# Dilated attention scores in one run over four PSUM banks, and the denominators as a full-array product

## The chip, the core and the metric

The kernel runs on one core of one Trainium2 chip. A core has TensorE (PE, matrix products), VectorE (DVE), ScalarE (ACT), GpSimd (POOL) and SyncE (SP), whose queue here issues the DMAs. The metric is the device time of one execution in microseconds; a profiled execution gives the trace that is read below. Lower is better.

## What is computed

A two-layer encoder trunk over 512 tokens of width 1024, all in float32. Each layer makes one big input projection, then three token mixers (a gated recurrence, a dilated sliding-window attention with 8 heads, a latent attention), gates, projects and merges them. The change touches the dilated attention alone. Cut to what matters:

```python
def _dilated_group(q, k, v, slopes, window, dilation):
    ...
    s = jnp.einsum('brnqhd,brnkhd->brhnqk', qb * (Dh ** -0.5), kb) + bias
    s = jnp.where(allowed, s, MASK_VALUE)
    m = jnp.max(s, axis=-1, keepdims=True)
    p = jnp.exp(s - m)
    den = jnp.sum(p, axis=-1, keepdims=True)
    o = jnp.einsum('brhnqk,brnkhd->brhnqd', p, vb) / den
    lse = (m + jnp.log(den))[..., 0]
    ...
def _dilated_mixer(qkv_groups):
    ...                          # three groups: dilation 1, 4 and 16
    w = jax.nn.softmax(jnp.stack(lses), axis=0)
    o = jnp.sum(w[..., None] * jnp.stack(outs), axis=0)
```

The softmax over the three groups means that one common maximum and one common denominator per query and head are enough.

## The kernel before

The projections (`in_fm`, `mm3`, line L300) keep features on the 128 partitions and 512 tokens on the free axis. A weight tile of 128 columns is loaded by SP (L280), ACT casts it to a high half (`w_...h`, L274), POOL subtracts to get the low half (`w_...l`, L275), and PE makes three passes of eight 128x512 products (`xh,h`, `xl,h`, `xh,l`). Two raw tiles and three split tiles are in flight.

The dilated stage runs over four head pairs, hp0 to hp3, in each of two layers: eight units. The main loop issues, for each pair, the scores (`dil_scores`), then the projections of the next pair (`dl`, or after hp3 the latent attention's `cq`, `ckv`, `kr` from `mla_compress`), then the exponentials (`dil_exp`), some of the merge (`br`, L1089, with the merge gates `mg`), and the values (`dil_values`).

In `dil_scores` a head has 64 features, so the two heads of a pair sit in the two halves of the partitions and their products use 64 rows of the array each (`dsa`, L927, for the first group; `dsb`, L951, for the other two). The products of the two heads are issued in turn, and go to two PSUM banks. DVE then adds the position table and takes the row minimum (L898), which leaves scores in `za`, `zb` and minima in the small tile `dst`. There are four such runs a unit: two for `dsa`, two for `dsb`, each of eight to sixteen 64-row passes (a float32 product counts as two), each after the minima that free its banks (`after(first, reads[-2])`).

The minima of the two sides have other token orders. So they are written to DRAM (`da` L984, `db` L974) and read back as `dso` (L985, L986, and L976 to L978), all on SP's queue. `dil_exp` takes the minimum of `dst` and `dso` (L993, DVE) and then makes 16 exponentials on ACT (L999, L1004). `dil_values` transposes them (`dta`, `dtb`), multiplies by the values into the output bank (`do`, L1019, two heads in two column halves of the array), and makes `dn` (L1063): the reciprocals of the denominators are spread over the partitions by a product with the identity, 64 columns for each head. Then `yb` = dn x gate x do (DVE).

PSUM has three pools here: four banks `mm` for the projections, three banks `at` (`at_bank`) for scores, transposes, `dn` and the norm broadcasts (`hgrb`, `cqrb`, L546), and one output bank (`o_bank`). Behind hp3 stands the norm of `cq`: `cqms` (L536, mean square by product), an inverse square root on DVE in three Newton steps (`rsqrt`, L261 to L267, tile `cqrs0y` or `cqrs1y` by layer), and `cqrb`, which spreads it over the partitions on PE.

The order of the instructions on each engine isn't the order of the code. A scheduler places them by a simulated timeline (`schedule_with_timeline_sim=True`), and `after(a, b)` adds an order between two instructions. A change of one stage can so move the work around it.

Of the kernel before, what the change touches and what calls it, by code (L numbers as in the profile page):

```python
# [195 lines left out]
def bcast(ap, dims):  # L196
    return bass.AP(ap.tensor, ap.offset, [list(ap.ap[0])] + [list(d) for d in dims])
# [3 lines left out]
def tile_encoder(ctx: ExitStack, tc: tile.TileContext, x, xt, positions, blocks, wuq, wuh, par_in, brow, lbp,  # L201
# [259 lines left out]
    def layer(l, x_src, need_next):  # L461
# [361 lines left out]
        def hgrn_pair(hp, parts, v):  # L823

            o = o_bank(f"ho{hp}_{l}")
            n = 0
            for w in range(NT):
                ws = slice(w * 128, w * 128 + 128)
                for what in range(3):
                    if (what == 1 and w == 0) or (what == 2 and w == 3):  # L830
                        continue
                    for i, (a, s, qq, ready) in enumerate(parts):
                        if what == 0:
                            c = 128 * hp + 64 * i
# [12 lines left out]
            sq = t2(f"hsq{hp}_{l}", tag="acc")  # L847
            A.activation(sq, o, AF.Square, scale=1.0 / KEY_SCALE)
            if hp == 0:
                squares.append(sq)  # L850
            else:
                V.tensor_tensor(squares[0], squares[0], sq, ALU.add)
            return oc
# [31 lines left out]
        def dil_scores(hp, qk):  # L885

            q0, k0, q1, k1, q2, k2 = qk
            sl = slopes()
            stat = sm.tile([128, 2, 2, 4], F32, tag="dst", name=f"dst{hp}_{l}")
            other = sm.tile([128, 2, 2, 4], F32, tag="dso", name=f"dso{hp}_{l}")  # L890
            za = [fap(t4(f"za{hp}{i}_{l}", tag="a4"), 0, [[1, 1024]]) for i in range(2)]
            zb = [fap(t4(f"zb{hp}{i}_{l}", tag="a4"), 0, [[1, 1024]]) for i in range(2)]
            tab_mid = con[:, O_MID:O_MID + 256]
            tab_end = con[:, O_END:O_END + 128]
            tab_b = con[:, O_G12:O_G12 + 256]

            def biased_min(dst, ps, tab, slope, acc):
                return V.tensor_tensor_reduce(dst, ps, tab, float(slope), 3.0e38, ALU.add, ALU.min, acc)  # L898


            pr = [slice(64 * i, 64 * i + 64) for i in range(2)]
            reads = []

            def pair(name, products, minima):
                sc = [at_bank(f"{name}{i}_{l}") for i in range(2)]
                first = products(sc)
                if reads:
                    after(first, reads[-2])
                if len(reads) > 2:
                    after(first, reads[-3])  # L910
                for i in range(2):
                    reads.append(minima(i, sc[i]))

            def products_a(jp):
                def go(sc):
                    first = None
                    for j in (2 * jp, 2 * jp + 1):
                        o_ = [t[:, (j % 2) * 256:(j % 2) * 256 + 256] for t in sc]
                        if j < 3:
                            ops = [(slice(0, 128), 256, slice(64 + 128 * j, 192 + 128 * j),  # L920
                                    slice(128 * j, 128 * j + 256))]
                        else:
                            ops = [(slice(0, 64), 128, slice(448, 512), slice(384, 512)),
                                   (slice(64, 128), 128, slice(0, 64), slice(0, 128))]
                        for rows, wd, qs, ks in ops:
                            for i in range(2):
                                m = nc.tensor.matmul(o_[i][rows, :wd], q0[pr[i], qs], k0[pr[i], ks], start=True,  # L927
                                                     stop=True)
                                first = first or m
                    return first  # L930
                return go

            def minima_a(jp):
                def go(i, ps):
                    for j in (2 * jp, 2 * jp + 1):
                        wd = 256 if j < 3 else 128
                        last = biased_min(za[i][:, 256 * j:256 * j + wd],
                                          ps[:, (j % 2) * 256:(j % 2) * 256 + wd], tab_mid if j < 3 else tab_end,
                                          sl[2 * hp + i], stat[:, 0, i, j:j + 1])
                    return last  # L940
                return go

            def products_b(rp):
                def go(sc):
                    first = None
                    for r in (2 * rp, 2 * rp + 1):
                        rs = slice(128 * r, 128 * r + 128)
                        for g, (q_, k_) in enumerate(((q1, k1), (q2, k2))):
                            c = (r % 2) * 256 + 128 * g
                            for i in range(2):  # L950
                                m = nc.tensor.matmul(sc[i][:, c:c + 128], q_[pr[i], rs], k_[pr[i], rs], start=True,  # L951
                                                     stop=True)
                                first = first or m
                    return first
                return go

            def minima_b(rp):
                def go(i, ps):
                    for r in (2 * rp, 2 * rp + 1):
                        last = biased_min(zb[i][:, 256 * r:256 * r + 256],  # L960
                                          ps[:, (r % 2) * 256:(r % 2) * 256 + 256], tab_b, sl[8 + 2 * hp + i],
                                          stat[:, 1, i, r:r + 1])
                    return last
                return go

            for jp in range(2):
                pair(f"dsa{hp}{jp}", products_a(jp), minima_a(jp))
            da = dram.tile([2, 576], F32, tag="da", name=f"da{hp}_{l}")
            db = dram.tile([2, 512], F32, tag="db", name=f"db{hp}_{l}")
            by_residue(da, stat, other)  # L970
            for rp in range(2):
                pair(f"dsb{hp}{rp}", products_b(rp), minima_b(rp))

            nc.sync.dma_start(db.rearrange("i (p r) -> p i r", r=4), stat[:, 1])  # L974
            for i in range(2):
                nc.sync.dma_start(other[:, 0, i, 0:3], db[i, 64:448].rearrange("(j p) -> p j", p=128))  # L976
# [33 lines left out]
        def dil_values(hp, exps, vs, gate, behind):  # L1010
# [46 lines left out]
            d = V.tensor_tensor(den[:, 1], den[:, 1], other[:, 1], ALU.add)  # L1057
            after(d, *copies)
            V.reciprocal(den[:, 1], den[:, 1])
            dn = at_bank(f"dn{hp}_{l}")  # L1060
            for r in range(4):
                for i in range(2):
                    nc.tensor.matmul(dn[64 * i:64 * i + 64, slice(r, None, 4)],  # L1063
                                     bcast(den[:, 1, i, r:r + 1], [[0, 64]]), ident, start=r == 0, stop=r == 3,
                                     skip_group_check=True)
            y = t2(f"yb{hp}_{l}")
            V.tensor_tensor(y, dn, gate, ALU.mult)
            V.tensor_tensor(y, y, o, ALU.mult)
            return split(y, f"yb{hp}{l}")


# [229 lines left out]
```

## Time and profile before

| | us |
|---|---|
| median of three runs | 1773.09 (1772.72 to 1774.57) |
| the profiled execution | 1771.63 |
| its span, granted TensorE clock | 1769.9, 0.996 |
| PE busy | 1741.8 (98%), 10616 matmuls |
| DVE, ACT, POOL busy | 1064.2 (60%), 730.3 (41%), 573.8 (32%) |
| DMA | 154.15 MB, mean 87 GB/s |

A row of the timeline gives the start in the span, the time of that group, the engine, the line, the operation with out<-in, shapes (rows*columns of the array, then partitions x elements), and in brackets the idle time of the engine before it with what ended it. Matmuls are pipelined: a row's time runs to the end of the last product, so the distance of two starts is the better price. PEld is PE's weight load, SPq is SP's DMA queue. "x16" counts passes. Tile names are without buffer numbers.

### The profile page before, as it was taken

What the parts mean: (1) busy time and instruction counts of PE and PEld (TensorE: products, weight loads), DVE (VectorE), ACT (ScalarE), POOL (GpSimd) and SP (SyncE); (2) the same over time, 40 slices, a digit from 0 to 9 for tenths busy, and PEclk for the clock granted to TensorE, in tenths of its full rate; (3) what the DMA queues carried; (4) which work ended last, traced back from release to release, by engine and by line L of the source; (5) the groups of instructions that cost most, each with busy time, mean ns of one, the idle gap of its engine ahead of it and who ended that gap; (6) DMA issues with size and microseconds to landing.
All of it is one profiled execution on the core that took longest, in us unless ns stands there. A gap on an engine that the chain in (4) does not pass through costs nothing. (4 is left out here: it accounts for less than half of the span.)

```text
span 1769.9 us, 26458 instructions
## 1 busy us (share of the span) xinstructions
PE 1741.8 (98%) x10616; PEld 1450.5 (82%) x10616; DVE 1064.2 (60%) x1912; ACT 730.3 (41%) x1273; POOL 573.8 (32%) x338
## 2 busy tenths in 40 slices
PE   9999999999999999999999999999999999999997
PEld 7778978988888888887888888888888888888876
DVE  8888777443232566756777778775333324666576
ACT  6445454242424353433254455442424254444330
POOL 0412244233333233333213212532433332433341
PEclk9999999999999999999999999999999999999999
DMA  5223222223222222332332222222223221324221
GB/s 194 84 66 102 73 73 89 73 72 96 79 77 84 70 75 79 113 111 72 119 114 90 84 78 74 89 78 78 72 72 98 82 83 48 99 67 151 72 86 69
DMA packets 77146, 154.15 MB, mean 87 GB/s; under 512 B 37728, under 2 KB 37856, under 8 KB 77024
## 3 DMA queue, kind: packets, MB, share of 16 engines
q1 hardware_dynamic: 77024, 152.47, 27.9%
q8 instruction: 83, 1.36, 0.3%
q14 instruction: 39, 0.32, 0.1%
HBM read 148.15 MB, written 4.29 MB: 86 GB/s over the span
## 5 line engine op out<-in xcount | busy, mean ns | idle before, releaser
L775 DVE TENSOR_TENSOR kk<-kk,fr 128x512 f32<-128x512 f32 x96 | 94.0, 999 | 30.0 <-ACT kc L745 18.9
L696 POOL TENSOR_TENSOR qq<-hq,fr 128x1024 f32<-128x1024 f32 x16 | 42.5, 2654 | 201.6 <-DVE fr L689 181.9
L774 DVE TENSOR_TENSOR qq<-qq,fr 128x512 f32<-128x512 f32 x96 | 75.3, 797 | 16.9 <-POOL qq L696 15.2
L1079 DVE TENSOR_SCALAR mg<-mg 128x512 f32<-128x512 f32 x32 | 53.2, 1669 | 49.0 <-ACT mg L1078 48.9
L898 DVE CUSTOM_DVE_ANT_0 zb<-dsb,con 128x256 f32<-128x256 f32 x64 | 23.3, 421 | 46.4 <-PE dsb L951 46.3
L767 DVE COPY_PREDICATED ha<-mask,hs 64x256 f32<-64x256 uint8 (+1 forms) x80 | 40.4, 505 | 16.7 <-PE hs L757 15.6
L275 POOL TENSOR_TENSOR wb_1l<-wb_1r,wb_1h 128x1024 fp32r<-128x1024 f32 x12 | 29.5, 2460 | 63.6 <-ACT wb_1h L274 42.5
L275 POOL TENSOR_TENSOR wb_0l<-wb_0r,wb_0h 128x1024 fp32r<-128x1024 f32 x12 | 29.5, 2461 | 63.4 <-ACT wb_0h L274 42.4
L881 DVE TENSOR_SCALAR dl<-dl,par,con 128x512 f32<-128x512 f32 x24 | 25.8, 1075 | 38.0 <-PE dl L300 37.9
L735 POOL TENSOR_SCALAR_AFFINE_SELECT ha<-hc 128x256 f32<-128x256 f32 x32 | 13.8, 456 | 105.0 <-ACT hc L730 97.3
L658 ACT COPY mpt<-mtr 128x128 f32<-128x128 f32 x64 | 17.0, 266 | 74.4 <-DVE mpt L658 74.4
L757 PEld LDWEIGHTS hs<-qq,kc 128*64 128x64 f32 x1024 | 33.1, 137 | 16.2 <-issue 8.4
L999 ACT ACTIVATE za<-za,dst 128x256 f32<-128x256 f32 x64 | 30.0, 470 | 33.2 <-DVE dst L993 33.2
L757 PE MATMUL hs<-qq,kc 128*64 128x64 f32 x1024 | 38.0, 225 | 4.3 <-DVE qq L774 4.3
L716 POOL TENSOR_TENSOR hk<-kk,f 128x256 f32<-128x256 f32 x32 | 24.8, 775 | 51.5 <-DVE fr L778 51.5
L792 ACT COPY hkt<-hkt 128x384 f32<-128x384 f32 x32 | 15.3, 480 | 59.9 <-PE hkt L790 59.6
L745 ACT COPY kc<-kk 128x512 f32<-128x512 f32 x64 | 37.5, 618 | 4.6 <-DVE kk L775 4.6
L658 DVE COPY mpt<-mtr 128x128 f32<-128x128 f32 x64 | 18.4, 288 | 32.7 <-PE mtr L655 22.3
L1079 DVE TENSOR_SCALAR mgc<-mgc 128x512 f32<-128x512 f32 x16 | 22.9, 1429 | 22.3 <-ACT mgc L1078 22.3
L1099 DVE TENSOR_TENSOR acc<-acc,mgc 128x512 f32<-128x512 f32 x16 | 32.2, 2049 | 0.0
L662 PE MATMUL mo<-mpt,mv 128*128 128x128 f32 (+1 forms) x192 | 31.9, 309 | 0.0
L1004 ACT ACTIVATE zb<-zb,dst 128x256 f32<-128x256 f32 x64 | 31.6, 495 | 0.0
(1509 smaller groups left out, 5400.8 us busy)
## 6 DMA issues: line engine op xcount, KB each, us to landing
wb_0r<-in_blocks_dram SPq DMA_DIRECT2D x12, 512.0 KB, 3.6
wb_1r<-in_blocks_dram SPq DMA_DIRECT2D x12, 512.0 KB, 3.6
w_0r<-in_blocks_dram SPq DMA_DIRECT2D x9, 512.0 KB, 3.4
w_1r<-in_blocks_dram SPq DMA_DIRECT2D x8, 512.0 KB, 3.6
w_2r<-in_blocks_dram SPq DMA_DIRECT2D x8, 512.0 KB, 3.5
w_3r<-in_blocks_dram SPq DMA_DIRECT2D x8, 512.0 KB, 3.6
wo_0r<-in_blocks_dram SPq DMA_DIRECT2D x8, 512.0 KB, 3.6
wo_1r<-in_blocks_dram SPq DMA_DIRECT2D x8, 512.0 KB, 3.5
```

The source lines that it names most:

```text
L275: (eng or nc.gpsimd).tensor_tensor(lo, raw, hi.bitcast(F32), ALU.subtract)
L658: (A.copy if kb % 2 else V.tensor_copy)(pts[kb][:, qs], tr[:, kb * 128:kb * 128 + 128])
L662: nc.tensor.matmul(o[:, cols], v[:, kb, h * 128:h * 128 + 128], pts[kb][:, cols], start=qt == 1 and kb == 0, stop=qt == NT - 1 and kb == N ...
L696: nc.gpsimd.tensor_tensor(qq, bcast(q, [[0, 2], [1, S]]), fr, ALU.mult)
L745: made = A.copy(fap(kc, 0, [[2 * m, R // 2], [m, 2], [1, m]]), fap(kk, 0, [[2 * m, R // 2], [S + m, 2], [1, m]]))
L757: mat = nc.tensor.matmul(sc[rows, to], kc[:, at], rhs, start=True, stop=True)
L767: ready = [V.copy_predicated(fap(a[rows], cols.start, [[128, NT], [1, wd]]), bcast(mk, [[0, NT], [1, wd]]), fap(sc[rows], cols.start, [[12 ...
L774: V.tensor_tensor(fap(qq, 0, dims), fap(qq, 0, dims), qf, ALU.mult)
L775: V.tensor_tensor(fap(kk, 0, dims), fap(kk, 0, dims), kf, ALU.mult)
L1004: A.activation(z, z, AF.Exp, bias=stat[:, 1, i, r:r + 1], scale=-1.0, accum_out=den[:, 1, i, r:r + 1])
L1079: V.tensor_scalar(g, g, 0.5, 0.5, ALU.mult, ALU.add)
L1099: V.tensor_tensor(acc[dt_], acc[dt_], g, ALU.add)
```

## The change

The two `dsa` runs of a unit become one run, and so do the two `dsb` runs (`side` in place of `pair`). A run now writes four banks: the three `at` banks and the output bank, which is free between the pair before's `yb` and this pair's `do`. The first product of a run waits for the last four reads of the run before, or for the last reader of the output bank (`newest["held_o"]`: hp0 takes the recurrence's square, the others the previous pair's `yb`).

For `dn`, the eight reciprocal columns are copied by ACT into a 128x512 tile `dr`, in which each of four column groups of 128 holds 64 copies for either head. Four full 128x128 products with the identity replace eight products with 64 columns. Lines behind the change move up by 12 or 13 (L993 becomes L980, L1063 becomes L1051, L1089 becomes L1076).

```diff
-            def pair(name, products, minima):
-                sc = [at_bank(f"{name}{i}_{l}") for i in range(2)]
-                first = products(sc)
-                if reads:
-                    after(first, reads[-2])
-                if len(reads) > 2:
-                    after(first, reads[-3])
-                for i in range(2):
-                    reads.append(minima(i, sc[i]))
+            def side(name, products, minima):
+                sc = [[at_bank(f"{name}0{i}_{l}") for i in range(2)], [at_bank(f"{name}10_{l}"), o_bank(f"{name}11_{l}")]]
+                after(products(sc), *reads[-4:], *([] if reads else newest["held_o"]))
+                for jp in range(2):
+                    for i in range(2):
+                        reads.append(minima(jp, i, sc[jp][i]))
...
-            for jp in range(2):
-                pair(f"dsa{hp}{jp}", products_a(jp), minima_a(jp))
+            side(f"dsa{hp}", products_a, minima_a)
...
-            for rp in range(2):
-                pair(f"dsb{hp}{rp}", products_b(rp), minima_b(rp))
+            side(f"dsb{hp}", products_b, minima_b)
...
             V.reciprocal(den[:, 1], den[:, 1])
+            dr = t2(f"dr{hp}_{l}", tag="f2")
+            A.copy(fap(dr, 0, [[128, 4], [64, 2], [1, 64]]), bcast(den[:, 1, 0, 0:1], [[1, 4], [4, 2], [0, 64]]))
             dn = at_bank(f"dn{hp}_{l}")
             for r in range(4):
-                for i in range(2):
-                    nc.tensor.matmul(dn[64 * i:64 * i + 64, slice(r, None, 4)],
-                                     bcast(den[:, 1, i, r:r + 1], [[0, 64]]), ident, start=r == 0, stop=r == 3,
-                                     skip_group_check=True)
+                nc.tensor.matmul(dn[:, slice(r, None, 4)], dr[:, 128 * r:128 * r + 128], ident, start=r == 0,
+                                 stop=r == 3, skip_group_check=True)
             y = t2(f"yb{hp}_{l}")
             V.tensor_tensor(y, dn, gate, ALU.mult)
-            V.tensor_tensor(y, y, o, ALU.mult)
+            newest["held_o"] = [V.tensor_tensor(y, y, o, ALU.mult)]
```

The scheduler places other work differently around it. Three places matter below.

First, PE at the scores of hp0 in layer 0. The numbers at the end of a name tell tiles apart; `hgrb` belongs to the recurrence, `dl` and `dg` are projections. Before:

```order
L300 MATMUL dl_3351<-xh,w_4224h 128x512 x2
L546 MATMUL hgrb_3081<-con,hgrs0y 128x128 x4
L927 MATMUL dsa_0_3283<-dl_0_2863 128x256
L927 MATMUL dsa_0_3284<-dl_0_2863 128x256
L927 MATMUL dsa_0_3283<-dl_0_2863 128x256
L927 MATMUL dsa_0_3284<-dl_0_2863 128x256
L300 MATMUL dl_3351<-xh,w_4224h 128x512 x6
L300 MATMUL dl_3351<-xl,w_4224h 128x512 x8
L300 MATMUL dl_3351<-xh,w_4224l 128x512 x8
L300 MATMUL dl_3383<-xh,w_4736h 128x512 x8
```

Now, the same place:

```order
L923 MATMUL dsa_0_3286<-dl_0_2863 128x256
L546 MATMUL hgrb_3081<-con,hgrs0y 128x128 x4
L923 MATMUL dsa_0_3283<-dl_0_2863 128x256
L923 MATMUL dsa_0_3284<-dl_0_2863 128x256
L923 MATMUL dsa_0_3283<-dl_0_2863 128x256
L923 MATMUL dsa_0_3284<-dl_0_2863 128x256
L923 MATMUL dsa_0_3286<-dl_0_2863 64x128 x2
L300 MATMUL dl_3351<-xh,w_4224h 128x512 x8
L300 MATMUL dl_3351<-xl,w_4224h 128x512 x8
L300 MATMUL dl_3351<-xh,w_4224l 128x512 x7
L923 MATMUL dsa_0_3285<-dl_0_2863 128x256
L923 MATMUL dsa_0_3285<-dl_0_2863 64x128 x2
```

Here the run of four banks is split: the product into the output bank (3286) starts ahead of `hgrb`, its partner (3285) comes 23 projections later. The `dsb` products of hp0 follow in two pieces, four products of one bank, ten projections, then eight products in pairs and four of one bank. In hp1 to hp3 each side is one piece, and 26 projections stand between `dn` and it.

Second, PE at hp2's merge in layer 0; `br` is the branch product, `wb_0h` and `wb_0l` are the halves of its weights. Before:

```order
L300 MATMUL mg_4805<-xh,w_11328l 128x512 x8
L1089 MATMUL br_0_4839<-ya00h,wb_0h 128x512
L1089 MATMUL br_0_4840<-ya00h,wb_0h 128x512
L300 MATMUL cq_5047<-xh,w_9216h 128x512 x8
L1089 MATMUL br_0_4839<-ya00h,wb_0l 128x512
L1089 MATMUL br_0_4839<-ya00l,wb_0h 128x512
```

Now:

```order
L300 MATMUL mg_4801<-xh,w_11328l 128x512 x8
L1076 MATMUL br_0_4835<-ya00h,wb_0h 128x512
L1076 MATMUL br_0_4835<-ya00h,wb_0l 128x512
L1076 MATMUL br_0_4835<-ya00l,wb_0h 128x512
L1076 MATMUL br_0_4835<-ya10h,wb_0h 128x512
L1076 MATMUL br_0_4835<-ya10h,wb_0l 128x512
```

The eight projections that stood between the high and the low half have moved behind the branch products. hp1 has the same move, with `mg` in the place of `cq`. On SP the loads of `wb` and of the weights behind it stand behind `db` there, and in hp3 one of two weight loads has moved from ahead of `db` to behind it.

Third, behind hp3 in layer 0: DVE at the inverse square root of `cq`. Before:

```order
L582 SCALAR_TENSOR_TENSOR krr_5296<-kr_5271,par_161,krt 128x512
L267 SCALAR_TENSOR_TENSOR cqrs0y<-cqrs0t,cqrs0y 128x4
L265 TENSOR_TENSOR cqrs0t<-cqrs0y 128x4
L266 TENSOR_TENSOR cqrs0t<-cqrs0t,cqrs0h 128x4
L267 SCALAR_TENSOR_TENSOR cqrs0y<-cqrs0t,cqrs0y 128x4
L993 TENSOR_TENSOR dst_0_4974<-dst_0_4974,dso_0_4975 128x2x4 x2
```

Now:

```order
L267 SCALAR_TENSOR_TENSOR cqrs0y<-cqrs0t,cqrs0y 128x4
L265 TENSOR_TENSOR cqrs0t<-cqrs0y 128x4
L266 TENSOR_TENSOR cqrs0t<-cqrs0t,cqrs0h 128x4
L980 TENSOR_TENSOR dst_0_4968<-dst_0_4968,dso_0_4969 128x2x4 x2
L267 SCALAR_TENSOR_TENSOR cqrs0y<-cqrs0t,cqrs0y 128x4
L582 SCALAR_TENSOR_TENSOR krr_5290<-kr_5265,par_161,krt 128x512
```

The two `dst` instructions have moved ahead of the last Newton step. PE at the same place, before:

```order
L300 MATMUL mg_5365<-xh,w_9920h 128x512 x8
L300 MATMUL mg_5365<-xl,w_9920h 128x512 x6
L536 MATMUL ckvms_5242<-con,ckvq_0_5204 128x1 x4
L300 MATMUL mg_5365<-xl,w_9920h 128x512 x2
L300 MATMUL mg_5365<-xh,w_9920l 128x512 x3
L546 MATMUL cqrb_5329<-con,cqrs0y 128x128 x4
```

Now:

```order
L300 MATMUL kr_5265<-xl,krw0h 128x512 x8
L300 MATMUL kr_5265<-xh,krw0l 128x512 x8
L300 MATMUL mg_5359<-xh,w_9920h 128x512 x5
L536 MATMUL ckvms_5236<-con,ckvq_0_5198 128x1 x4
L546 MATMUL cqrb_5323<-con,cqrs0y 128x128 x4
L300 MATMUL mg_5359<-xh,w_9920h 128x512 x3
```

`cqrb` has moved up by fourteen projections. Layer 1 has the same rows at this place on both engines.

More of the change, by code (lines that the diff above doesn't have):

```diff
@@ L847, in hgrn_pair @@
             sq = t2(f"hsq{hp}_{l}", tag="acc")
-            A.activation(sq, o, AF.Square, scale=1.0 / KEY_SCALE)
+            newest["held_o"] = [A.activation(sq, o, AF.Square, scale=1.0 / KEY_SCALE)]
             if hp == 0:
@@ L902, in dil_scores @@
             reads = []
-            def pair(name, products, minima):
-                sc = [at_bank(f"{name}{i}_{l}") for i in range(2)]
-                first = products(sc)
-                if reads:
-                    after(first, reads[-2])
-                if len(reads) > 2:
-                    after(first, reads[-3])
-                for i in range(2):
-                    reads.append(minima(i, sc[i]))
[L914 to L925, printed above, removed]
-                            for i in range(2):
[L927 to L964, printed above, removed]
-            for jp in range(2):
-                pair(f"dsa{hp}{jp}", products_a(jp), minima_a(jp))
+            def side(name, products, minima):
[4 more added lines that the diff above has]
+                        reads.append(minima(jp, i, sc[jp][i]))
@@ new lines, in products_a @@
+            def products_a(sc):
+                first = None
+                for j in range(4):
+                    o_ = [t[:, (j % 2) * 256:(j % 2) * 256 + 256] for t in sc[j // 2]]
+                    if j < 3:
+                        ops = [(slice(0, 128), 256, slice(64 + 128 * j, 192 + 128 * j),
+                                slice(128 * j, 128 * j + 256))]
+                    else:
+                        ops = [(slice(0, 64), 128, slice(448, 512), slice(384, 512)),
+                               (slice(64, 128), 128, slice(0, 64), slice(0, 128))]
+                    for rows, wd, qs, ks in ops:
+                        for i in range(2):
+                            m = nc.tensor.matmul(o_[i][rows, :wd], q0[pr[i], qs], k0[pr[i], ks], start=True,
+                                                 stop=True)
+                            first = first or m
+                return first
@@ new lines, in minima_a, with products_b @@
+            def minima_a(jp, i, ps):
+                for j in (2 * jp, 2 * jp + 1):
+                    wd = 256 if j < 3 else 128
+                    last = biased_min(za[i][:, 256 * j:256 * j + wd],
+                                      ps[:, (j % 2) * 256:(j % 2) * 256 + wd], tab_mid if j < 3 else tab_end,
+                                      sl[2 * hp + i], stat[:, 0, i, j:j + 1])
+                return last
+            def products_b(sc):
+                first = None
+                for r in range(4):
+                    rs = slice(128 * r, 128 * r + 128)
+                    for g, (q_, k_) in enumerate(((q1, k1), (q2, k2))):
+                        c = (r % 2) * 256 + 128 * g
+                        for i in range(2):
+                            m = nc.tensor.matmul(sc[r // 2][i][:, c:c + 128], q_[pr[i], rs], k_[pr[i], rs], start=True,
+                                                 stop=True)
+                            first = first or m
+                return first
@@ L968, in dil_scores, with minima_b @@
+            def minima_b(rp, i, ps):
+                for r in (2 * rp, 2 * rp + 1):
+                    last = biased_min(zb[i][:, 256 * r:256 * r + 256],
+                                      ps[:, (r % 2) * 256:(r % 2) * 256 + 256], tab_b, sl[8 + 2 * hp + i],
+                                      stat[:, 1, i, r:r + 1])
+                return last
+            side(f"dsa{hp}", products_a, minima_a)
             da = dram.tile([2, 576], F32, tag="da", name=f"da{hp}_{l}")
@@ L1059, in dil_values @@
             V.reciprocal(den[:, 1], den[:, 1])
+            dr = t2(f"dr{hp}_{l}", tag="f2")
+            A.copy(fap(dr, 0, [[128, 4], [64, 2], [1, 64]]), bcast(den[:, 1, 0, 0:1], [[1, 4], [4, 2], [0, 64]]))
             dn = at_bank(f"dn{hp}_{l}")
             for r in range(4):
-                for i in range(2):
-                    nc.tensor.matmul(dn[64 * i:64 * i + 64, slice(r, None, 4)],
-                                     bcast(den[:, 1, i, r:r + 1], [[0, 64]]), ident, start=r == 0, stop=r == 3,
-                                     skip_group_check=True)
+                nc.tensor.matmul(dn[:, slice(r, None, 4)], dr[:, 128 * r:128 * r + 128], ident, start=r == 0,
+                                 stop=r == 3, skip_group_check=True)
             y = t2(f"yb{hp}_{l}")
             V.tensor_tensor(y, dn, gate, ALU.mult)
-            V.tensor_tensor(y, y, o, ALU.mult)
+            newest["held_o"] = [V.tensor_tensor(y, y, o, ALU.mult)]
             return split(y, f"yb{hp}{l}")
```

## The prediction

> **What bounds the kernel now.** I read the page's busy table first, then the engine's waits, then the timeline of PE through one head pair, then the queue of SP and the DVE rows behind it.
>
> ```profile
> PE 1741.8 (98%) x10616; PEld 1450.5 (82%) x10616; DVE 1064.2 (60%) x1912; ACT 730.3 (41%) x1273; POOL 573.8 (32%) x338
> ...
> PE cq L300 <- ACT mg L1078: 1.0, 2, 0.6
> ```
>
> PE is busy for 98% of the span and the largest waits elsewhere are not in the dilated stage, so a microsecond that PE spends here is a microsecond of the time, and so is any wait that is put in PE's way. In the dilated stage PE waits twice, 1.0 us in all, at the second row. A change of order can therefore cost more than the switches that it saves. All prices below are from the profiled execution (1771.63 us, span 1769.9); it stands 1.46 us under the median of the runs, 1773.09, and I add the sum to the median.
>
> **What a score run costs.** The timeline of PE, second head pair of layer 0 (start, duration, line, operation):
>
> ```profile
> 431.19 1.04 PE L1063 MATMUL dn<-con,dden 128*64 128x128 f32 x16
> 432.17 1.13 PE L927 MATMUL dsa<-dl 64*128 64x256 f32 x8
> ...
> 434.49 1.98 PE L300 MATMUL dl<-xh,w_5888l 128*128 128x512 f32 x8
> 436.31 1.98 PE L300 MATMUL dl<-xh,w_6400h 128*128 128x512 f32 x8
> 438.21 1.08 PE L927 MATMUL dsa<-dl 64*128 64x256 f32 x12
> 439.23 2.11 PE L300 MATMUL dl<-xl,w_6400h 128*128 128x512 f32 x8
> 441.18 1.98 PE L300 MATMUL dl<-xh,w_6400l 128*128 128x512 f32 x8
> 442.99 1.52 PE L300 MATMUL dl<-xh,w_7424h 128*128 128x512 f32 x6
> 444.44 1.16 PE L951 MATMUL dsb<-dl 64*128 64x128 f32 x16
> 445.53 0.73 PE L300 MATMUL dl<-xh,w_7424h 128*128 128x512 f32 x2
> 446.10 2.00 PE L300 MATMUL dl<-xl,w_7424h 128*128 128x512 f32 x8
> ```
>
> Eight full projections take 436.31 - 434.49 = 1.82 us, 0.227 each. From 436.31 to 441.18 lie sixteen of them and the x12 run: 4.87 - 3.63 = 1.24 us. From 441.18 to 446.10 lie sixteen and the x16 run: 4.92 - 3.63 = 1.29. What of that is streaming, two narrower answers of the timeline show:
>
> ```profile
> 366.88 0.50 PE L951 MATMUL dsb<-dl 64*128 64x128 f32 x6
> ...
> 367.32 0.50 PE L951 MATMUL dsb<-dl 64*128 64x128 f32 x6
> ...
> 350.79 0.50 PE L546 MATMUL hgrb<-con,hgrs0y 128*128 128x128 f32 x3
> ...
> 351.01 0.50 PE L546 MATMUL hgrb<-con,hgrs0y 128*128 128x128 f32 x3
> ...
> L546 PEld LDWEIGHTS hgrb<-con,hgrs0y x8: 188/190/192, 350.5 to 351.4; 128*128 128x128 f32 x8
> ```
>
> Four pairs of 64-row passes start within 0.44 us, so a pair takes 0.11 and sixteen matmuls take 0.88; entering and leaving the 64-row mode is the other 0.41 us of a run, and 0.82 of the x12 run is streaming. A full-array fp32 pass over 128 columns (hgrb) takes 0.11 as well, as long as a pair.
>
> **Pairs hp1 to hp3 (six units): a gain.** Four runs become two: -2 x 0.41 = -0.82. dn took 432.17 - 431.19 = 0.98 in sixteen column-half passes, without a change of mode behind do; now eight full passes, 8 x 0.11 = 0.88, stand between do and projections, and the exit from the half-array mode, until now shared with the dsa run, becomes dn's own. Between nothing and half a run's 0.41 I take 0.2, so dn with its switch is +0.1, and with the later entry of dsa +0.2. A unit saves about 0.6, six units -3.6 us (bounds -4.9 and -2.5). The dn of hp3 has no score run beside it: within 0.1, left out.
>
> **Pair hp0 (two units): a loss.** By the order, the third score bank is still hgrb's when hp0's scores start, so the one run of a side falls apart: the product in the output bank goes alone, then hgrb, then the first pair, later the fourth product alone, and side b likewise. Before, there were four runs of paired passes; now five, in which the second half of each side goes unpaired. A lone 64-row pass occupies the array as long as a pair, by the 0.11 that even a full pass takes, so the second x12 run's 0.82 of streaming is done twice (+0.75, since four quadrant passes still go two by two) and dsb's second half too (8 x 0.11 = +0.88); the fifth run is +0.41. That is +2.0 a unit, +4.1 for both layers. [...] PE's own work therefore changes by about -3.6 + 4.1 = +0.5 us: the saved switches are given back.
>
> The LDWEIGHTS row (min/median/max ns) shows full-array loads of 190 ns behind passes that start every 110 ns: they overlap, though rows and array are the same. [...]
>
> **dr, the copies, and the loads.**
>
> ```profile
> 425.29 0.20 DVE L1059 RECIPROCAL dden<-dden 128x8 f32<-128x8 f32 x1
> ...
> L745 ACT COPY kc<-kk 128x512 f32<-128x512 f32 x64 | 37.5, 618 | 4.6 <-DVE kk L775 4.6
> ```
>
> The eight copies to dr are ACT work of about 0.62 us each (the copy of the same shape). The reciprocal ends at 425.5 and dn starts at 431.19: 5.7 us cover the copy and a weight cast ahead of it, and ACT is at 41%. I cost them at nothing; if that cover were gone, 0.6 us per pair would show. The first dsa matmul's new wait for yb (or hp0's square) costs nothing: in the new order 26 projections, 5.9 us, lie between dn and dsa. Where hp0's later weight loads are moved past db on SP, their casts keep some 5 us.
>
> **hp3: the largest term.** The accumulators of the minima go out by SP and come back (da, db, dso), then DVE takes the final minimum dst, then ACT's exponentials start. SP's rows, layer 1 and for da layer 0, with hp2's dn, which I call T:
>
> ```profile
> 1460.99 1.04 PE L1063 MATMUL dn<-con,dden 128*64 128x128 f32 x16
> ...
> 1469.82 0.93 SPq L984 DMA_DIRECT2D da<-dst  x2
> 1480.84 0.33 SPq L985 DMA_DIRECT2D dso<-da  x1
> ...
> 1481.76 1.40 SPq L280 DMA_DIRECT2D w_11456r<-in_blocks_dram  x1
> ...
> 1483.68 0.42 SPq L974 DMA_DIRECT2D db<-dst  x1
> 1488.57 0.91 SPq L976 DMA_DIRECT2D dso<-db  x2
> ...
> 594.03 0.93 SPq L984 DMA_DIRECT2D da<-dst  x2
> 602.62 0.33 SPq L985 DMA_DIRECT2D dso<-da  x1
> ...
> db<-dst SPq DMA_DIRECT2D x8, 4.0 KB, 4.5
> ```
>
> And what stands behind on DVE and PE:
>
> ```profile
> 1482.43 0.42 DVE L898 CUSTOM_DVE_ANT_0 zb<-dsb,con 128x256 f32<-128x256 f32 x1
> ...
> 1482.78 0.42 DVE L898 CUSTOM_DVE_ANT_0 zb<-dsb,con 128x256 f32<-128x256 f32 x1
> ...
> 1486.85 0.16 DVE L267 SCALAR_TENSOR_TENSOR cqrs1y<-cqrs1t,cqrs1y 128x4 f32<-128x4 f32 x1
> ...
> 1492.50 0.24 DVE L993 TENSOR_TENSOR dst<-dst,dso 128x8 f32<-128x8 f32 x2 [5.48 <-DMA dso<-db]
> ...
> 1488.58 0.94 PE L536 MATMUL ckvms<-con,ckvq 128*128 128x1 f32 x8
> ...
> 1490.64 1.05 PE L546 MATMUL cqrb<-con,cqrs1y 128*128 128x128 f32 x8
> ```
>
> Before, the last step of the reciprocal root, cqrs1y, ends at 1487.0, and cqrb comes at 1490.64, 3.6 us later: dst may wait 5.48 us for its DMA and nobody on PE notices. The new order puts both dst instructions ahead of that last step, and cqrb after only five of the mg products. So cqrb waits for cqrs1y, that waits on DVE behind dst, and dst waits for the DMA. Everything later on PE is queued behind cqrb.
>
> How long: from dn to cqrb now lie 90 projections (20.4 us), dn with its switch (1.1), the two merged runs (0.82 and 0.86 streaming for a, 1.79 for b, 0.41 twice: 4.3) and two groups of eight single-column passes (ckvms 0.94 busy, some 0.8 in the pipeline): T+27.5. The data come so: the dsa run starts at T+7.0 as its second half did (438.21 - 431.19), but all eight minima now follow it; four more at 0.35 (1482.78 - 1482.43) put da 1.3 us later, from T+8.83 to T+10.1. It lands 11.0 us later (1480.84 - 1469.82): T+21.2. Then the load w_11456r stands ahead of db (0.9 and 0.4): T+22.5. db takes 4.5 (the median row) to 4.9 (1488.57 - 1483.68): T+27.2. dst follows 3.9 behind (1492.50 - 1488.57): T+31.1, and 0.4 for dst and the last step: cqrb could start at T+31.5. PE stands 4.0 us in layer 1. In layer 0 da lands 2.4 us sooner (8.59 against 11.02), which leaves 1.6; db may be quicker too and I take 0.8. Sum +4.8, ends 0 and 7.5.
>
> **hp1 and hp2: one wait for another.**
>
> ```profile
> 1390.67 1.04 PE L1063 MATMUL dn<-con,dden 128*64 128x128 f32 x16
> ...
> 1422.68 0.51 ACT L999 ACTIVATE za<-za,dst 128x256 f32<-128x256 f32 x1 [5.30 <-DVE dst L993]
> ...
> 1432.05 2.37 POOL L275 TENSOR_TENSOR wb_1l<-wb_1r,wb_1h 128x1024 fp32r<-128x1024 f32 x1 [13.09 <-ACT wb_1h L274]
> ...
> 1432.31 0.61 PE L1089 MATMUL br<-ya01h,wb_1h 128*128 128x512 f32 x2
> 1433.56 2.11 PE L300 MATMUL cq<-xh,w_9216h 128*128 128x512 f32 x8 [0.64 <-ACT mg L1078]
> ```
>
> Now the second br product takes the low half of wb, which POOL finishes at 1434.42, 11.74 after the first exponential, with ACT's cast behind all sixteen. Before, eight projections covered it, at the price of cq's waits: 1433.56 - 1432.31 = 1.25 for two products of 0.227, 0.8 lost where the row counts 0.64. By that measure the 1.0 of the first fence is 1.25, and with shorter ones too short for that view I estimate 1.5. br reached T+41.64 and now comes 0.6 sooner, the second product 0.23 later: T+41.3. In layer 1 the first exponential was at T+32.0; with db some 0.3 sooner and without the wb load beside it, T+30.8, so the low half is ready at T+42.5: 1.2 a unit, 2.4 for two. In layer 0, with da 2 us quicker, 0.1. Net 2.5 - 1.5 = +1.0, ends -1.5 and +3.
>
> **The sum:** +0.5 (PE's own), +4.8 (hp3), +1.0 (hp1, hp2) = +6.3, on 1773.09: 1779.4 us. A measurement of this kernel can tell about 0.2%, 3.5 us, from no change.
>
> **The rivals.** *The stall does not come* (25%). If dst is done by T+27.0, cqrb waits for nothing. That asks 4 us less on the da-db chain in layer 1, for instance da landing as soon as in layer 0 (8.59) and db 1.6 us sooner than its row. Then 0.5 + 1.0 and up to 1.6 are left: +1 to +3, 1774 to 1776, the same. For it speaks that one queue entry fewer stands ahead of db, against it that SP's rows repeat from pair to pair. *Faster* (10%). Lone passes of hp0 run in the shadow of their neighbours: the extra run alone, 0.8 for both units instead of 4.1. PE's own work is then -2.8; with hp1's and hp2's old waits gone and their new one absent, -1.5 more, and no hp3 stall: -4.3, 1768.8. It decides only if dst also comes before T+27. The trace holds no lone 64-row pass; the nearest, hgrb's full ones at 0.11, speak against it. *Lone weight loads exposed* (10%): hp0 has 24 lone passes a layer; each with up to 0.08 (190 - 110) more is 1.9 a unit, 3.8 in all: +10.1, 1783.2. [...] *My forecast* (55%): 1776.6 to 1782.5 by itself.
>
> **Range and chances.** The low end takes in most of the missing stall and part of the faster case, 1772; the high end the exposed loads or a longer da, 1784. Faster by over 0.2%: 10%. Within: 28%, the missing stall and the low edge of the forecast. Slower: 62%.
>
> **What would show it.** Right: in hp3 PE's wait at cqrb on DVE cqrs, about 4 us in layer 1 and less in layer 0; dst rows unmoved or earlier than before against the clock, and the old 5.48 idle in front of them shorter; PE's busy time within 1 us of 1741.8; five score runs in hp0 with lone passes every 0.11; br waiting for POOL wb in layer 1 where cq waited for ACT. Wrong: cqrb without a wait, lone passes faster or slower than 0.11, dn later than its dr, or dsa waiting for yb.

## The result, and the profile after

The changed kernel takes 1815.45 us (median of four runs, 1813.01 to 1815.90) against 1772.9 us before: a ratio of 1.0242 (95% interval 1.0227 to 1.0258), some 43 us slower. The forecast was 1779.4 us with a range up to 1784: the direction was right, the size was not. The profiled execution has a span of 1813.6 us at a mean granted clock of 0.986 (before: 1769.9 and 0.996).

The busy row and the waits of PE of the changed kernel (waited for: us in total, times, longest):

```profile
PE 1756.8 (97%) x10552; PEld 1463.6 (81%) x10552; DVE 1070.4 (59%) x1912; ACT 733.3 (40%) x1281; POOL 578.6 (32%) x338
...
PE dta L1017 <- DVE dta20p L1022: 14.4, 2, 7.4
PE mg L300 <- ACT mg L1065: 6.8, 2, 3.4
...
PE cqrb L546 <- DVE cqrs1y L267: 3.4, 1, 3.4
...
PE br L1076 <- POOL wb_1l L275: 1.5, 2, 0.8
...
PE cqrb L546 <- DVE cqrs0y L267: 0.9, 1, 0.9
```

Of these 43 us, cqrb's waits and br's were forecast. The first two rows were not: 21.2 us, once in hp2 (dta) and once in hp1 (mg) of each layer. And PE is busy for 15.0 us longer (1756.8 - 1741.8) with fewer matmuls, where I had said within 1 us.

**The score runs came out as priced.** PE in hp1 and in hp0 of layer 0, after:

```profile
433.45 1.16 PE L1051 MATMUL dn<-con,dr 128*128 128x128 f32 x8
434.37 1.41 PE L300 MATMUL dl<-xl,w_5888h 128*128 128x512 f32 x5
...
440.47 1.95 PE L923 MATMUL dsa<-dl 64*128 64x256 f32 x20
```

```profile
350.43 0.70 PE L923 MATMUL dsa<-dl 64*128 64x256 f32 x2
...
352.15 1.50 PE L923 MATMUL dsa<-dl 64*128 64x256 f32 x12
...
359.01 1.06 PE L923 MATMUL dsa<-dl 64*128 64x256 f32 x6
...
365.85 2.05 PE L943 MATMUL dsb<-dl 64*128 64x128 f32 x24
```

To see where time goes I compared the start of the same projection in both traces, at some twenty places in each layer. Across hp0's scores the changed kernel falls back by 2.05 us in either layer (forecast 2.0); across the scores of hp1 and of hp2 it gains 0.61 each time (forecast 0.6). dn starts 0.92 us ahead of the next projections (434.37 - 433.45); before, it started 0.98 ahead of the dsa run that followed it. The whole of the loss, cut at the same marks: hp0 +4.1; the scores of hp1 and hp2 -2.4; the rest of hp1 +6.9 and +7.1; hp2 from its merge to the root of hp3, hp3's scores included, +8.4 and +10.8; from cqrb on +2.7 and +5.7. With -0.2 between the stages that is 43.0, the distance of the two last matmuls (1801.84 and 1758.79).

**What stands in the way in hp1 and hp2 is on SP.** SP's queue in hp2 of layer 0, before and then after:

```profile
543.88 0.53 SPq L280 DMA_DIRECT2D w_9216r<-in_blocks_dram  x1
548.84 2.23 SPq L984 DMA_DIRECT2D dd<-dden  x2
559.64 0.33 SPq L985 DMA_DIRECT2D dso<-dd  x1
```

```profile
554.71 0.36 SPq L971 DMA_DIRECT2D dd<-dden  x1
555.16 0.46 SPq L280 DMA_DIRECT2D w_9216r<-in_blocks_dram  x1
556.57 0.36 SPq L971 DMA_DIRECT2D dd<-dden  x1
573.24 0.33 SPq L972 DMA_DIRECT2D dso<-dd  x1
...
574.17 0.36 SPq L280 DMA_DIRECT2D w_9344r<-in_blocks_dram  x1
```

`dd` is the third round trip of a unit: the denominators of one side go to DRAM in two writes and come back in the other token order. In the new order a weight load of 512 KB stands between the two writes, w_9216r in hp2 and w_10944r in hp1. From the first dd to its reading back was 10.8 us (559.64 - 548.84) and is 18.5 (573.24 - 554.71). The load itself suffers too. The page's DMA rows (KB, then median us from issue to landing), before and after:

```profile
w_10944r<-in_blocks_dram SPq DMA_DIRECT2D x2, 512.0 KB, 3.9
w_9216r<-in_blocks_dram SPq DMA_DIRECT2D x2, 512.0 KB, 3.9
```

```profile
w_10944r<-in_blocks_dram SPq DMA_DIRECT2D x2, 512.0 KB, 12.2
w_9216r<-in_blocks_dram SPq DMA_DIRECT2D x2, 512.0 KB, 13.9
```

The trace's single packets show in what order the three transfers went. All three use one queue (q1). The packets of 4 bytes of the first dd start at 555.6 to 556.0. The load's 128 packets of 4 KB start at 556.5 to 566.6, where those of wb_0r just before took from 551.9 to 554.1. The packets of the second dd, issued at 556.57, start only at 565.8, when 89 of the load's have started, and it lands at 573.10. In the kernel before, the second dd's packets start 0.9 us after its issue. Why the load's packets take ten microseconds behind the first dd is not shown.

The next load, w_9344r, goes out behind dso, at 574.17 (dso at 573.24), and everything behind it is late. ACT, DVE and PE after:

```profile
578.00 1.04 ACT L274 CAST w_9344h<-w_9344r 128x1024 fp32r<-128x1024 f32 x1 [9.16 <-DMA w_9344r<-in_blocks_dram]
578.95 0.68 ACT L1065 ACTIVATE mg<-mg,hpar 128x512 f32<-128x512 f32 x1
```

```profile
579.66 2.08 DVE L1066 TENSOR_SCALAR mg<-mg 128x512 f32<-128x512 f32 x1 [8.65 <-ACT mg L1065]
...
582.87 0.68 DVE L1022 COPY dta20p<-dta 128x512 f32<-128x512 f32 x1
```

```profile
575.10 1.07 PE L300 MATMUL cq<-xh,w_9216l 128*128 128x512 f32 x4
583.60 0.90 PE L1017 MATMUL dta<-con,za 128*128 128x128 f32 x3 [7.43 <-DVE dta20p L1022]
```

ACT's cast of the late weight stands ahead of the merge gate on ACT's queue; DVE takes the gate ahead of the copy of the transposed scores; PE needs that copy's bank. So a transfer of 2 KB holds PE for 7.4 us, through three engines' queues.

**And PE comes back at half speed.** PE behind hp1's stall, and one window of 10 us (its length, busy us of PE, PEld, DVE, ACT and POOL, the granted clock, DMA share, GB/s):

```profile
489.17 3.78 PE L300 MATMUL mg<-xh,w_11072h 128*128 128x512 f32 x8 [3.42 <-ACT mg L1065]
492.75 3.21 PE L300 MATMUL mg<-xl,w_11072h 128*128 128x512 f32 x8
495.80 1.98 PE L300 MATMUL mg<-xh,w_11072l 128*128 128x512 f32 x8
```

```profile
490.00:500.00 10.00, 10.00 (x34) 7.95 (x34) 5.54 (x5) 3.32 (x5) 7.39 (x4) 0.73 0.45 123
```

Eight products take 3.58 us (492.75 - 489.17) and then 3.05, where they took 1.82. The window's clock of 0.73 says the same. Fourteen products go at 0.44 us each: 3.0 us on top of a stall of 3.4. Most of the 15 us of busy time is this, behind the five longest of the stalls above, and no work is in it.

### The profile page after: what moved, and what is told of

It reads as the page before. It is cut to its first block, busy times and chain, and to the rows that moved or that the text cites. A ratio compares the mean times of both kernels' runs of the same rounds, so it can differ in the third digit from the quotient of the medians.

```text
span 1813.6 us, 26334 instructions
## 1 busy us (share of the span) xinstructions
PE 1756.8 (97%) x10552; PEld 1463.6 (81%) x10552; DVE 1070.4 (59%) x1912; ACT 733.3 (40%) x1281; POOL 578.6 (32%) x338
## 4 chain that ended last, share of the span: by engine, by line
PE 73%; DMA 10%; DVE 9%; ACT 3%; issue 2%; POOL 2%; SPq 1%; DVEq 0%; ACTq 0%; POOLq 0%
PE mg L300 13%; PE dl L300 10%; PE dv L319 8%; PE hf L300 6%; PE br L1076 5%; PE hq L300 3%; DMA dd<-dden 3%; PE hgg L300 2%; PE wo L1237 2%; PE do L1006 2%; DMA da<-dst 2%; PE cq L300 1%; DVE kk L775 1%; PE hs L757 1%; DMA db<-dst 1%
## 5 line engine op out<-in xcount | busy, mean ns | idle before, releaser
L767 DVE COPY_PREDICATED ha<-mask,hs 64x256 f32<-64x256 uint8 (+1 forms) x80 | 40.4, 506 | 16.7 <-PE hs L757 15.5
```

Source lines behind the costliest of these rows:

```text
L767: ready = [V.copy_predicated(fap(a[rows], cols.start, [[128, NT], [1, wd]]), bcast(mk, [[0, NT], [1, wd]]), fap(sc[rows], cols.start, [[12 ...
```

## The experiments

The tile names are those of the code; each time stands beside runs of the kernel before on the same chip. `order(a, b)` puts a behind b on its engine without a wait.

### The load behind both dd writes

```diff
+        if name.split("_")[-1] in ("10944", "9216") and newest.get("dd"):
+            order(d, *newest["dd"])
```

> The changed kernel with one thing moved: on SP the weight load that stood between the two dd writes of hp1 and hp2 (w_10944r, w_9216r, both layers) now stands behind both; four places, all other queues as in the changed kernel. Theory A (the load between the two writes makes dd land 7 us late, SP is held at the read-back of dd, the next weight loads come late, PE waits 3.5 us in hp1 and 7.4 us in hp2 and then runs some 3 us worth of half clock): dd to dso<-dd falls from about 18 to about 11 us, those waits fall to under 1 us each, 2 x (3.5 + 3.0) + 2 x (7 + 3) = 33 us come back: about 1782 us (1778 to 1788). What remains over before is hp0 (+4.1), cqrb in hp3 (4.3 plus its cold clock) and br. Rival B (the merged score runs make da and db late, and everything behind the exponentials with them): the waits stay, 1811 to 1816 us. Rival C (the copies to dr hold ACT's queue): the waits stay, 1811 to 1816.

1795.68 us, ratio 1.0124 (1.0108 to 1.0139). Four swaps of neighbours on SP, and nothing else, give 20 of the 43 us back. The dd trip falls to 11.3 to 12.2 us. I had expected 1782. Now the load is what comes late (behind both writes it lands after 13.1 and 13.4 us by the median), and that holds PE as well:

```profile
PE dta L1025 <- DVE dta20p L1030: 3.2, 2, 1.9
...
PE mg L307 <- ACT mg L1073: 3.0, 2, 1.7
```

### The same fault in the kernel before

The kernel before with the load behind the first dd write, `order(d, newest["dd"][0])`, and all else as it was.

> The kernel before with the mirror move: the same four weight loads, which stood ahead of the two dd writes, now stand between them; all other queues as before, scores in pairs, dn as before. Theory A: dd to dso<-dd rises from about 10.5 to about 18 us; w_11072r and w_9344r are issued 7 us later; PE waits 3 to 5 us in hp1 and 5 to 7 us in hp2 and loses about 3 us more each time by the clock: +25 to +36 us, about 1803 us. Rivals B and C: nothing that they name is in this kernel: 1771 to 1776 us.

1806.21 us, ratio 1.0181 (1.0165 to 1.0196). So 33 us of loss come from the place of four loads, without any merged run. The dd trip is 18.9 to 19.1 us, and PE waits where the old order has its weights:

```profile
PE cq L307 <- ACT mg L1086: 13.2, 2, 7.1
PE mg L307 <- ACT mg L1086: 11.8, 2, 6.4
```

### The scores alone, and dn alone

scores_only is the changed kernel with dn as before; dn_only is the kernel before with the copies to dr and the four full-array products.

> Only the score part of the change: one run a side over four banks; dn with its sixteen half-column passes as before. The queues stand as in the changed kernel, but for dn and the copies. Theory A and rival B: the whole loss is here, 1812 to 1817 us. Rival C (copies to dr): the waits are gone, 1773 to 1785 us. The difference to the changed kernel is the price of the dn part, which I put at 0 to +1.5 us in all.

> Only the dn part of the change: copies to dr and four full products; scores in four runs as before. The queues stand as in the kernel before, but for dn, the copies and, behind hp3, the place of dn against the mvps products. Theory A and rival B: 1772 to 1775 us, the same as before. Rival C: over 1800 us.

scores_only takes 1825.88 us, ratio 1.0288 (1.0271 to 1.0304); dn_only 1772.65, ratio 0.9994 (0.9984 to 1.0003). The loss belongs to the scores, and beside scores in four runs dn is worth nothing. That the scores alone lose 10 us more than the whole change was not expected. The changed kernel again, on another chip than that of scores_only:

> The changed kernel once more, on the chip of the other runs of this call, to have a scale for them: 1813 to 1826 us. If it comes near the 1826 of the run with the scores alone, that run's distance to 1815 was the chip's; if it comes near 1815, the dn part is worth 10 us.

1817.4 us, ratio 1.026 (1.0246 to 1.0274): the changed kernel differs by 2 us between its two measurements, not by 10. What the chip of scores_only does to it was not measured, so a share of that chip is not excluded. In scores_only the dd trip is 19.2 to 19.7 us; the two profiles of the changed kernel have 17.7 to 18.6 and 18.3 to 19.4, and before_load_between, on the chip of scores_only, 18.9 to 19.1. By the marks, scores_only loses 11.5 us more than the first profile of the changed kernel; 1.8 of that lie ahead of the dilated stage and 4.4 in hp1 of layer 0.

### The loads ahead of both dd writes

```diff
+        for held in newest.get("ahead", {}).pop(name.split("_")[-1], ()):
+            order(held, d)          # held: the two dd writes
```

> The changed kernel with the same four weight loads (w_10944r, w_9216r) issued ahead of both dd writes instead of between them, as in the kernel before; all other queues as in the changed kernel, br and cqrb included. Theory A: dd to dso<-dd is 10 to 11.5 us and these loads land in 4 us instead of 12; the waits for mg's ACT and for dta that were left with the load behind both writes (3.0 and 3.2 us) go too; what stays is br for the low half of wb (about 4 us), cqrb (about 5 us and its cold clock) and hp0 (+4.1): 1785 to 1792 us. Rival B (the merged runs' late da and db are what holds the exponentials): no better than with the load behind, 1794 to 1798.

1784.7 us, ratio 1.0081 (1.0065 to 1.0096), 0.3 under the range that I expected: 33 us of the changed kernel's loss are gone with four swaps on SP. The loads land in 4.2 and 4.6 us, the dd trip takes 10.2 to 11.1, dta and mg wait for nothing. Of what is left, PE's waits show:

```profile
PE cqrb L553 <- DVE cqrs1y L272: 3.3, 1, 3.3
...
PE br L1084 <- POOL wb_1l L280: 2.4, 2, 1.2
...
PE cqrb L553 <- DVE cqrs0y L272: 1.2, 1, 1.2
```

### dn again, with the queue in order

load_ahead_dd with dn as before the change. The order is otherwise the same on PE, POOL and SP; on ACT and DVE a few steps change places.

> load_ahead_dd (1784.7) with dn as before the change (sixteen half-array passes, no dr copies), everything else in the same order on every engine. Theory (dn costs and gains nothing in either order): 1783 to 1787. Rival (the copies to dr and the shorter dn are worth some 8 us once the scores are merged, as the distance of scores_only, 1825.9, to the changed kernel, 1817.4, would have it): 1791 to 1795, then with longer waits between dn and yb or at the score runs.

1783.27 us, ratio 1.0071 (1.0058 to 1.0083). dn is neutral here too, so it does not explain the 10 us of scores_only.

### hp0's scores in runs of two banks again

load_ahead_dd, with `side` for hp1 to hp3 alone and the old `pair` for hp0.

> The loads stand ahead of both dd writes as in load_ahead_dd (1784.7), and in addition hp0's scores go back to runs of two banks; hp1 to hp3 and dn stay as changed. Theory (the lone 64-row passes and the fifth run of hp0 cost 2.05 us of PE's time in each layer, and nothing of it is hidden): 1784.7 - 4.1 = 1780.6, with the landmark behind hp0 at +0.0 against before, and the waits behind hp3 unchanged. Rival (hp0's passes only fill time in which PE would wait later, since cqrb behind hp3 waits for a chain that starts anew in each pair): 1783 to 1786, with longer waits in hp0 or hp1.

1778.54 us, ratio 1.0039 (1.0026 to 1.0051): 6 us less than load_ahead_dd. Across hp0's scores PE now loses 0.00 us in both layers, so the lone passes and the fifth run had cost their full 4.1; three of hp0's weight loads on SP move as well, and the waits at cqrb and br are somewhat shorter.

### Two attempts on the wait at cqrb

ahead_root is load_ahead_dd with hp3's dst held behind the last Newton step:

```diff
+                if hp == 3:
+                    order(m, newest["cq_root"])
```

> load_ahead_dd (1784.7) with the two dst instructions of hp3 held behind the last Newton step of cq's root. Theory A (cqrb's wait and the slow PE behind it are all that is lost there): the waits of 3.3 and 1.2 us and the 1.7 to 2.0 us of slow matmuls behind each go, 1784.7 - 8 = 1776 to 1778. Theory B (the exponentials' chain, 1.3 us later in each merged unit, has no slack; without the stall at cqrb PE meets it a little later, at dta or dtb of hp3): 1781 to 1784, with a wait of 2 to 5 us at dta, dtb or the products behind them in hp3.

1786.1 us, ratio 1.0081 (1.0067 to 1.0095): nothing is gained. cqrb no longer waits, and the wait turns up later in hp3, longer. The row of waits, and DVE in layer 1:

```profile
PE dta L1029 <- DVE ckvc L576: 8.1, 2, 5.4
```

```profile
1500.03 0.24 DVE L989 TENSOR_TENSOR dst<-dst,dso 128x8 f32<-128x8 f32 x2 [6.54 <-DMA dso<-db]
...
1509.50 2.47 DVE L596 TENSOR_TENSOR krq<-krr,krs 64x512 f32<-64x512 f32 x1 [3.49 <-ACT krs L595]
```

DVE stands at dst until dso is there, then ACT makes the exponentials, and the latent attention's krs comes behind them on ACT; so DVE stands a second time, and its next steps, ckvc among them, reach PE 5.4 us late. The other way was to bring the loads of wb ahead of db as well, which puts cqrb behind nineteen mg products as before:

> The changed kernel with, besides, the wb load of hp1 and hp2 issued ahead of db, as in the kernel before; the scheduler then puts the projections back between br's high and low half and cqrb back behind nineteen of the mg products, so PE's order at both places is nearly that of before. Scores and dn as in the changed kernel. Theory A (the whole loss beyond PE's own work is the order of loads and what the order moved): +4.1 for hp0, -3.6 for hp1 to hp3, some 1 to 2 us left at cqrb, since dst still stands ahead of one or two Newton steps: 1773 to 1778 us. Rival B: 1790 us or more.

1786.82 us, ratio 1.0087 (1.0073 to 1.0101), 9 above the range that I expected. In layer 1 dst still stands ahead of the last two Newton steps; DVE waits 5.7 us there for db, and PE then waits 3.8 us at cqrb. With this and both repairs above together:

> As the run with all loads ahead, and two things more: hp0 keeps its scores in four runs of two banks (no lone passes), and in hp3 dst stands behind the last Newton step of cq's root. dn as in the changed kernel. Theory A with my prices of PE's own work: hp0 +0, hp1 to hp3 -3.6, no stall at cqrb: 1768 to 1771 us, faster than before by 0.15 to 0.3%. Rival (the merged runs gain nothing on the chip): 1772 to 1776.

1783.63 us, ratio 1.0068 (1.0055 to 1.008), a miss of 13. Each cure moved the wait:

```profile
PE dta L1040 <- DVE ckvc L576: 3.9, 2, 2.5
PE mg L307 <- ACT mg L1088: 1.6, 2, 0.8
```

### Only side b merged

In the merged units da goes out 10.2 us behind dn instead of 8.8, since all eight minima now follow the whole run. If that lateness is what moves from wait to wait, it should go when side a is back in two runs:

> hp0_pairs_root (1783.6) with side a of hp1 to hp3 back in two runs; only the dsb runs are merged, dn stays as changed. Theory B (the merged dsa run makes da, and with it the exponentials, 1.3 us late, and this chain has no slack): da stands again as in before against dn, the waits in hp1, hp2 and hp3 that hp0_pairs_root showed go, and PE saves some 0.2 to 0.4 us a unit: 1770 to 1774. Rival C (the waits come from the other orders that the scheduler chose, not from a's lateness): 1780 to 1784.

1781.32 us, ratio 1.0057 (1.0045 to 1.007): the number of the rival. The trace gives another reason for it. The scheduler took dsb apart, eight of its passes going alone between those of dsa:

```profile
438.04 0.37 PE L963 MATMUL dsb<-dl 64*128 64x128 f32 x1
438.05 0.48 PE L943 MATMUL dsa<-dl 64*128 64x256 f32 x1
...
445.33 2.05 PE L963 MATMUL dsb<-dl 64*128 64x128 f32 x24
```

The score runs of hp1 and of hp2 cost +0.85 us against the kernel before where they gained 0.61. da is back at 8.7 us behind dn, and the rest of hp1 and hp2, four units together, is 5.2 us shorter than in hp0_pairs_root. So for hp1 and hp2 the late da is supported, not cleanly shown, for the order changed too; in layer 1 some 3 us are still lost from the root of cq on, and those it does not explain.

### hp1 and hp2 alone merged

> ahead_hp0_pairs (1778.5 beside 1771.35 of the kernel before) with hp3's scores back in runs of two banks as well; only hp1 and hp2 are merged, dn stays as changed. The root of cq then comes ahead of dst again. Theory (of the 7 us that remained, all lies behind hp3, in cqrb's wait and the slow matmuls behind it; hp1 and hp2 by themselves give 4 x 0.61 = 2.4 us and lose some 1.7 to the wait of br for POOL's wb): within 1.5 us of the kernel before, 1770 to 1773, no wait at cqrb, br waiting 1 us at most in a unit. Rival (the merged units of hp1 and hp2 carry a loss of their own further on, in hp3's queue): 1775 or more, with a wait at dta or dtb of hp3.

> The same with the wb load ahead of db too, so that PE's order at br is as before the change. Theory (da, 1.3 us late in a merged unit, then shows as waits at mg, cq, br and dtb of hp1 and hp2, 1.2 to 1.6 and 0.6 to 1.1 us a unit as in hp0_pairs_root, 4.4 in all against the 2.4 saved): 2 us above the kernel before, 1772.5 to 1775. Rival (the waits of hp0_pairs_root came from hp3's or the root's new order): 1768.5 to 1771, faster than before.

ahead_hp12 (loads ahead of dd; hp0 and hp3 in the old runs) takes 1771.69 us, ratio 1.0003 (0.9994 to 1.0012); all_ahead_hp12 (with wb's loads ahead of db too) 1773.12, ratio 1.0009 (1.0 to 1.0018). Both times lie in the ranges of their theories, and the last 7 us of ahead_hp0_pairs lay in hp3. But neither kernel keeps the 2.4 us that four units with merged runs save on PE. In the one, br waits for POOL, up to 1.3 us where I had said 1 at most. In the other, whose profiled execution took 1776.13 us, 3 above the median, mg waits for ACT in hp1, and in layer 0 cqrb for dst:

```profile
PE br L1095 <- POOL wb_1l L280: 1.8, 2, 1.3
```

```profile
PE cqrb L553 <- DVE dst L998: 2.0, 1, 2.0
PE mg L307 <- ACT mg L1084: 1.6, 2, 0.8
```

No version here is faster than the kernel before.

## Why the prediction was right in direction and wrong in size

**Right: PE's own work.** Forecast -3.6 + 4.1 us; the marks show 0.61 a unit saved in hp1 and hp2 and 2.05 lost in each hp0, and ahead_hp0_pairs removed that. The lone passes of hp0 go at the 0.11 us taken for them: seven of dsb's start from 362.49 to 363.16, 0.11 apart, though dsb's weight loads take 188 ns by the median. So the rival with exposed weight loads (another 3.8 us) did not come.

**Right in mechanism, too small: hp3's chain.** With T = 1497.22, the start of dn in hp2 of layer 1:

```profile
1507.45 1.31 SPq L971 DMA_DIRECT2D da<-dst  x2
1518.28 0.33 SPq L972 DMA_DIRECT2D dso<-da  x1
...
1519.63 0.42 SPq L961 DMA_DIRECT2D db<-dst  x1
1523.82 0.90 SPq L963 DMA_DIRECT2D dso<-db  x2
```

```profile
1527.81 0.24 DVE L980 TENSOR_TENSOR dst<-dst,dso 128x8 f32<-128x8 f32 x2 [5.94 <-DMA dso<-db]
```

da goes out at T+10.2 (forecast 10.1), is read back at T+21.1 (21.2), db goes at T+22.4 (22.5), dst comes at T+30.6 (31.1). cqrb waits 3.4 and 0.9 us (forecast 4.0 and 0.8). But from cqrb to the end of hp3 the loss is 5.7 and 2.7, not 4.0 and 0.8. In layer 1 the rest is half speed behind the stall: 2.3 us, cqrb's own products included. In layer 0 there is a second wait, 1.0 us at ckvrb, and some 0.8 that is not traced. None of these was a term of the sum. ahead_root showed that the wait is not cqrb's alone: taken away there, it comes back at dta.

**Right, but too small to matter:** br's wait (0.8 a time, forecast 1.2 in layer 1), dr's copies hidden, dn.

**Wrong: "hp1 and hp2: one wait for another", net +1.0.** This is the step that failed; the marks put 33 us there (6.9 + 7.1 + 8.4 + 10.8, hp3's scores included). The waits at mg and dta are 21.2 of it, and the half speed behind them makes up most of the rest. I followed the moved loads of wb to br and stopped. The first part of the document says that the weight loads behind wb also moved behind db, and I priced only hp0's casts for it. Where the next load then stood, between the two dd writes, I did not look, though SP's order showed it ahead of time. load_behind_dd, load_ahead_dd and above all before_load_between show that this one place carries 20 to 33 us.

**Wrong: a stall was priced at its own length.** The trace of before held the counter-evidence. PE's timeline of the kernel before, early in layer 0:

```profile
65.99 3.75 PE L300 MATMUL hq<-xh,w_256h 128*128 128x512 f32 x8 [3.32 <-ACT w_2304h L274]
69.54 3.11 PE L300 MATMUL hq<-xl,w_256h 128*128 128x512 f32 x8
```

A stall of 3.32 us, then eight products in 3.55 us, 2.9 us too much over fourteen of them. It lay outside the dilated stage and I passed over it. In the changed kernel the stalls at mg (3.4 and 3.3 us), at dta (7.4 and 7.0) and at cqrb in layer 1 (3.4) thus cost 3.0, 3.0, 2.0, 2.6 and 2.3 us on top, some 13 in all.

**What stays open.** Why some 3 us stay in layer 1 from the root of cq on with da on time (b_merged); why scores_only loses 10 us more than the changed kernel, with the same order on PE and SP; and what makes the load behind dd slow.

## What to carry to other kernels

When a change moves a load on an engine's issue queue, look at what it now stands between: here a weight load put between two writes of one round trip delayed the trip (10.8 to 18.5 us in hp2 of layer 0), the load (3.9 to 12.2 and 13.9 by the median), and every load behind the read-back, and PE paid for it through the queues of ACT and DVE. Price a stall of PE with the slow stretch behind it (here 2.0 to 3.0 us), and look in the trace of before for an example of one. And a gain on the busiest engine (here 3.7 us at best, 0.2%) is kept only where the chains that feed it have slack; merging runs that free that engine also made their results 1.4 us late, and the waits took it back.

## What the hardware showed that I had not expected

**A load queued behind small writes.** A write of 2 KB in 4-byte pieces (dd) lands after 8.1 us in the kernel before and 9.0 in the changed kernel, by the medians of sixteen. A 512 KB load issued behind it on the same queue lands after 11.9 to 15.8 us (the changed kernel, load_behind_dd and before_load_between), where it takes 3.8 to 4.8 when issued ahead (the kernel before and load_ahead_dd). In the changed kernel a second dd write behind that load is read back 15.9 to 16.7 us later, where 8.1 to 8.9 pass in the kernel before; in the packets above the second dd starts nine microseconds after its issue, among the load's last. No run put the load on another queue.

**PE at half speed after a pause.** In the trace of the kernel before PE pauses once for 3.0 us or more (start to start, past the first 10 us), in that of the changed kernel six times, for 3.4 to 7.8 us. Behind each of these seven pauses the full-width products start some 0.44 us apart instead of 0.227, at 2.0 to 3.0 us in all. Behind the 22 pauses of 1.0 to 1.85 us (9 and 13) none do, and neither trace has one between 1.85 and 3.4. My count over all sixteen traces (the changed kernel has two) is not as clean: 39 of 41 pauses of 3.0 us or more, 5 of ten between 2.0 and 3.0, and 7 of 195 of 1.0 to 1.85 are followed by half speed, so here the length of the pause alone does not decide it. In the record of the granted clock, in the two traces, each of the seven has one stretch at 0.50, six of 6.83 us and one of 10.24, and up to the last matmul there is no other. The stretch begins 1.6 to 4.9 us into the pause, and what a pause costs goes with what is left of it: at mg in hp1 of layer 0 it lies from 488.52 to 495.35 and PE is back at 489.17, with 6.2 us left; at dta in hp2 it lies from 580.68 to 587.51 and PE is back at 583.60, after the longer pause, with 3.9 left.
